# Bias rows written to HBM in 32 shifted copies instead of 128, and read back in parts of 32 partitions

## The chip, the core and the metric

The kernel runs on one core of a Trainium2 chip. The metric is the device time of one execution in microseconds (us). TensorE does the matmuls, VectorE and ScalarE the elementwise work, and 16 DMA engines move data between HBM and the on-chip memory SBUF. DMAs are issued by SyncE (most of them) and by ScalarE; in the profile the two issuing queues are called SPq and ACTq.

## The reference

The reference is a transformer block (two attentions, cross attention, a gated feed-forward) followed by a second block with a recurrent mixer and 64 experts. The change concerns the relative bias of the first block's attentions alone. Both attentions, 8 and 4 heads, add to each logit a value that depends on the distance of query and key:

```python
bias_ht = table_a.T.astype(jnp.float32)
logits = logits + bias_ht[h_i[..., None], rel_bucket(dist)]
mask = slot_ok[None, :, :, None] & (dist >= 0)
logits = jnp.where(mask, logits, NEG_INF)
```

So for each head there is one row of 384 numbers by distance (with the mask in it), and query p of a block of 128 needs 256 of them, starting one place further left than query p - 1 does.

## The kernel before

Weights pass through a stream of pages (128 partitions x 2048 floats, 1 MB). SyncE loads a page (line 220); ScalarE copies it rounded (`wh`, line 246) and VectorE takes the difference (`wl`, line 247); TensorE then multiplies in three passes (lines 643 to 645). `ws512` handles a block of 512 output columns with the weights stationary, in two half blocks (chunks) of one page each and 48 matmuls of 256 columns; `ts512` does the same with the activations stationary. The first blocks are `w_in` columns 512, 0, 1024, 2048, 1536 and 2560. The program's order is written out by hand, engine by engine.

The start of the program: `cols`, `xT` and the first `w_in` page are loaded in pieces (lines 474 to 479), then two more pages (482), `x`, `misc`, `diff_lambda`, `bsp` (from `b_spatial`, line 494) and `brow` (from `b_router`, line 496). For the bias, TensorE multiplies the table with a one-hot matrix (line 710), which gives the 12 rows `bv`; VectorE copies them to SBUF (`bvs`, a part of the page `tmp`, line 711). One DMA from ScalarE's queue (line 715) then writes every row 128 times into the HBM scratch `bd`, copy r shifted by r floats. In the loop around it ScalarE and VectorE convert the first activations and the first weight page, slice by slice (`gain`, line 580 and 581, and `split`, line 575 and 576).

After the third block's matmuls in the program, two SyncE DMAs read `bd` back so that partition p holds its row shifted by p: `biasA` for 8 heads, `biasB` for 4 (line 778). Behind them SyncE loads `memT` and `mem` (lines 892, 894) and the further weights. The attention adds `biasA` to the logits (line 809), takes the maxima (811) and exponentials (813), and TensorE transposes the result (832).

A DMA signals its end on one of eight completion semaphores, DMAHW0 to DMAHW7, which the DMAs of both queues take in rotation. A DMA that takes a semaphore waits first until its previous user has landed.

Of the kernel before, what the change touches and what calls it, by code (L numbers as in the profile page):

```python
# [10 lines left out]
F32 = mybir.dt.float32  # L11
# [312 lines left out]
def body(nc, tc, A, OUT, ctx, dbg=None):  # L324
# [8 lines left out]
    dr = ctx.enter_context(tc.tile_pool(name="dr", bufs=1, space=bass.MemoryType.DRAM))  # L333
# [50 lines left out]
    def w3(t, **kw):  # L384
        return t.rearrange("p (a b) -> p a b", **kw)
# [78 lines left out]
    oh, bvs = tmp0[0:33, 0:384], tmp0[0:12, 384:768]  # L464
# [35 lines left out]
    def gcol(key):  # L500
        a, n = COL[key]
        return [cols[:, i:i + 1] for i in range(a, a + n)]
# [71 lines left out]
    def split(hi, lo, src):  # L574
        S.activation(hi, src, AF.Copy)
        V.tensor_sub(lo, src, hi.bitcast(F32))
# [6 lines left out]
    def gain(parts, xT_, g, ks=range(8)):  # L583

        for k in ks:
            sl = slice(k * 256, k * 256 + 256)
            split_scaled(parts[0][:, sl], parts[1][:, sl], xT_[:, sl], g[k])
# [121 lines left out]
    bv = bank("bv")  # L709
    PE.matmul(bv[0:12, 0:384], tab, oh, start=True, stop=True)  # L710
    V.tensor_copy(bvs, bv[0:12, 0:384])
    bd = dr.tile([12, 128, 512], F32, name="bd")
    for i in range(4):
        if i == 2:
            nc.scalar.dma_start(bass.AP(tensor=bd.tensor, offset=bd.offset, ap=[[65536, 12], [513, 128], [1, 384]]),
                                bvs[:, None, :].to_broadcast([12, 128, 384]))
        s = slice(i * 512, i * 512 + 512)
        gain(hT, xT, gcol("mix_norm_g"), (2 * i, 2 * i + 1))
        split(c.hi[:, s], c.lo[:, s], c.raw[:, s])
# [55 lines left out]
    rel(tmp0)  # L775
    run_all(ts512(hT, "w_in", 1024, evac_v(vab[:, 0:1024], fx)))
    for t, h0, n in ((biasT[0], 0, 8), (biasT[1], 8, 4)):
        nc.sync.dma_start(w3(t[:, :n * 256], a=n), bass.AP(tensor=bd.tensor, offset=bd.offset + h0 * 65536 + 127,
                                                           ap=[[512, 128], [65536, n], [1, 256]]))

    def attention(diff, qk_, v, bias, out_cols):
        q, k = w3(qk_[:, 0:1024], a=4), w3(qk_[:, 1024:2048], a=4)
# [351 lines left out]
    def ffn_in():  # L1134
        hv = [w3(h, a=8) for h in nh["h"]]
        for u in range(11):
# [4 lines left out]
            for n in ("w_gate", "w_up"):  # L1141
# [3 lines left out]
                for k in range(8):  # L1145
# [5 lines left out]
                    if k == 3:  # L1151
# [18 lines left out]
                                                ap=[[0, 128], [1, 1024]]))  # L1170
# [6 lines left out]
    for u in range(11):  # L1177
# [3 lines left out]
        for tt, k2 in sorted(parts) if u == 10 else parts:  # L1181
            f = 2 * u + k2
            i, o = divmod(f * 256, 2048)
# [977 lines left out]
    bd = [mset.bank("ed") for n in range(2)]  # L2161
# [88 lines left out]
```

## Time and profile before

| | |
|---|---|
| median of 3 runs | 1227.41 us (1226.05 to 1227.77) |
| the profiled execution's own time | 1227.2 us |
| its span, first to last instruction | 1225.4 us |
| TensorE busy | 1166.3 us |
| VectorE busy | 632.9 us |
| ScalarE busy | 465.9 us |
| moved by DMA | 353.20 MB, mean 288 GB/s |

The span is shorter than the time by what lies around it, 1.8 us. A busy TensorE is not one at its peak: matmuls are pipelined, and the granted clock, 2.4 GHz or 1.2 GHz, stands in the profile as 1.00 or 0.50.

### The profile page before, as it was taken

Reading aid. Unit: us, or ns where it says so; the run is one execution under the profiler, and the core shown is the slowest. Engines: PE = TensorE matmul, PEld = TensorE weight load, DVE = VectorE, ACT = ScalarE, POOL = GpSimd, SP = SyncE. Lnnn points to the kernel's source line nnn. Section 1 sums busy time; section 2 is a strip of 40 time slices with the busy share of each in tenths; the row PEclk is TensorE's granted clock in tenths of the full one; section 3 lists DMA queues with packets and bytes.
Section 4 is the critical chain, followed back from the end, with each engine's and each line's share of the span. In section 5 each row is a group of like instructions: output and inputs, shape, how many; then the busy total and the mean of one; then the engine's idle time right before and its main releaser. Section 6 shows DMA issues by size and latency. Waiting matters only on the chain.

```text
span 1225.4 us, 18528 instructions
## 1 busy us (share of the span) xinstructions
PE 1166.3 (95%) x7391; PEld 837.5 (68%) x7391; DVE 632.9 (52%) x1280; ACT 465.9 (38%) x738; POOL 2.0 (0%) x9
## 2 busy tenths in 40 slices
PE   7989999999999999999999978999999999998986
PEld 6878987689999988998888757444444434442442
DVE  4568856465545446865686656343333323331333
ACT  4446535545534443777445433111111111110121
POOL 0000000000000000000000000000000000000000
PEclk9889999999999999999999988999999999999998
DMA  8853789644554665343355997899999999999994
GB/s 300 252 213 138 264 344 388 241 174 153 190 206 143 228 226 178 118 149 114 139 193 197 361 359 288 336 410 422 422 420 420 421 421 421 420 421 421 421 420 175
DMA packets 55152, 353.20 MB, mean 288 GB/s; under 512 B 6007, under 2 KB 9368, under 8 KB 13848
## 3 DMA queue, kind: packets, MB, share of 16 engines
q1 hardware_dynamic: 51984, 342.90, 70.7%
q10 hardware_dynamic: 3080, 9.10, 2.6%
q8 instruction: 59, 0.97, 0.3%
q14 instruction: 29, 0.24, 0.1%
HBM read 347.51 MB, written 4.46 MB: 287 GB/s over the span
## 4 chain that ended last, share of the span: by engine, by line
PE 70%; DMA 22%; DVE 4%; ACT 2%; issue 1%; SPq 0%; DVEq 0%; ACTq 0%
DMA w<-in_w_expert_gu 11%; PE gu L1940 8%; DMA w<-in_w_expert_down 6%; PE tsb L643 6%; PE tsb L645 6%; PE tsb L644 6%; PE ed L1969 5%; DMA w<-in_w_in 3%; PE ga L1909 3%; PE acc L1979 3%; PE ws L645 2%; PE ws L643 2%; PE ws L644 2%; PE w_up L643 2%; PE w_gate L643 2%; PE w_up L645 2%
## 5 line engine op out<-in xcount | busy, mean ns | idle before, releaser
L247 DVE TENSOR_TENSOR wl<-w,wh 128x1024 fp32r<-128x1024 f32 (+1 forms) x210 | 242.3, 1201 | 95.9 <-ACT wh L246 87.2
L246 ACT ACTIVATE wh<-w 128x1024 fp32r<-128x1024 f32 (+1 forms) x210 | 205.0, 1039 | 66.6 <-DMA w<-in_w_in 31.8
L1940 PE MATMUL gu<-w,xe 128*32 128x512 f32 (+1 forms) x1216 | 201.3, 594 | 11.8 <-DMA w<-in_w_expert_gu 11.8
L1940 PEld LDWEIGHTS gu<-w,xe 128*32 128x32 f32 (+1 forms) x1216 | 61.1, 121 | 147.5 <-issue 115.2
L1969 PE MATMUL ed<-w,hT 128*32 128x512 f32 (+1 forms) x608 | 109.0, 597 | 3.0 <-DMA w<-in_w_expert_down 2.9
L643 PE MATMUL ws<-hi,wh 128*128 128x256 f32 x352 | 104.1, 296 | 3.2 <-ACT wh L246 3.2
L645 PE MATMUL ws<-hi,wl 128*128 128x256 f32 x352 | 102.7, 292 | 1.6 <-DVE wl L247 1.2
L643 PE MATMUL tsb<-wh,hi 128*128 128x512 f32 x256 | 101.5, 397 | 2.1 <-ACT g1r L572 2.1
L644 PE MATMUL ws<-lo,wh 128*128 128x256 f32 x352 | 102.6, 292 | 0.5 <-DVE lo L581 0.5
L645 PE MATMUL tsb<-wh,lo 128*128 128x512 f32 x256 | 99.9, 390 | 0.0
L644 PE MATMUL tsb<-wl,hi 128*128 128x512 f32 x256 | 99.9, 390 | 0.0
L1949 DVE TENSOR_TENSOR hh<-hh,gu 128x256 f32<-128x256 f32 x27 | 11.4, 422 | 148.3 <-ACT hh L1948 148.3
L580 ACT ACTIVATE ey<-ed,ws 128x512 fp32r<-128x512 f32 x54 | 37.1, 687 | 122.4 <-PE ed L1969 122.4
L1948 ACT ACTIVATE hh<-gu 128x256 f32<-128x256 f32 x27 | 10.4, 383 | 188.2 <-PE gu L1940 188.2
L581 DVE SCALAR_TENSOR_TENSOR ey<-ed,ws,ey 128x512 fp32r<-128x512 f32 x54 | 40.5, 751 | 77.7 <-ACT ey L580 77.7
L643 PEld LDWEIGHTS ws<-hi,wh 128*128 128x128 f32 x352 | 70.6, 201 | 6.2 <-ACT wh L246 3.8
L1969 PEld LDWEIGHTS ed<-w,hT 128*32 128x32 f32 (+1 forms) x608 | 29.8, 121 | 64.8 <-issue 50.0
L645 PEld LDWEIGHTS ws<-hi,wl 128*128 128x128 f32 x352 | 70.3, 200 | 2.4 <-DVE wl L247 1.7
L644 PEld LDWEIGHTS ws<-lo,wh 128*128 128x128 f32 x352 | 70.5, 200 | 0.9 <-DVE lo L581 0.8
L1979 PE MATMUL acc<-ey,gt 128*128 128x512 f32 x216 | 60.0, 412 | 0.0
L643 PEld LDWEIGHTS tsb<-wh,hi 128*128 128x128 f32 x256 | 48.2, 188 | 11.8 <-ACT g1r L572 2.5
L1979 PEld LDWEIGHTS acc<-ey,gt 128*128 128x128 f32 x216 | 37.5, 188 | 27.4 <-issue 21.4
(450 smaller groups left out, 2116.5 us busy)
## 6 DMA issues: line engine op xcount, KB each, us to landing
w<-in_w_expert_gu SPq DMA_DIRECT2D x128, 1024.0 KB, 19.8
w<-in_w_expert_down SPq DMA_DIRECT2D x60, 1024.0 KB, 19.7
w<-in_w_in SPq DMA_DIRECT2D x39, 1024.0 KB, 7.0
w<-in_w_ada SPq DMA_DIRECT2D x24, 1024.0 KB, 7.2
w<-in_w_gate SPq DMA_DIRECT2D x11, 1024.0 KB, 4.9
w<-in_w_up SPq DMA_DIRECT2D x11, 1024.0 KB, 6.5
w<-in_w_down SPq DMA_DIRECT2D x11, 1024.0 KB, 5.0
w<-in_w_out SPq DMA_DIRECT2D x8, 1024.0 KB, 6.7
```

The lines of the kernel that those rows point to most:

```text
L246: kb.nc.scalar.activation(c.hi[:, s], c.raw[:, s], AF.Copy)
L247: kb.nc.vector.tensor_sub(c.lo[:, s], c.raw[:, s], c.hi[:, s].bitcast(F32))
L580: S.activation(hi, src, AF.Copy, scale=col)
L581: V.scalar_tensor_tensor(lo, src, col, hi.bitcast(F32), op0=OP.mult, op1=OP.subtract)
L643: PE.matmul(out, l[0], r[0], start=start, stop=False, skip_group_check=free)
L644: PE.matmul(out, l[0], r[1], start=False, stop=False, skip_group_check=free)
L645: PE.matmul(out, l[1], r[0], start=False, stop=stop, skip_group_check=free)
L1909: PE.matmul(b[:, i * w:i * w + w], xs[part][:, tt, dd * 128:dd * 128 + 128], oh_[:, tt, :], start=part + tt == 0, stop=part + tt == 2)
L1940: PE.matmul(b[w * e:w * e + w, :], xe[:, k, w * e:w * e + w], w3(gu[e][k // 4], a=4)[:, k % 4, :], start=k == 0, stop=k == 7, skip_group_c ...
L1949: V.tensor_mul(h, h, b[:, 256:512])
L1969: PE.matmul(b[w * e:w * e + w, :], hT_[:, f * 128 + w * e:f * 128 + w * e + w], w3(dn[e], a=2)[:, f, n * 512:n * 512 + 512], start=f == 0, ...
L1979: PE.matmul(sums[tt, n], gt[:, tt * 128:tt * 128 + 128], y[:, part * 1024 + n * 512:part * 1024 + n * 512 + 512], start=False, stop=stop a ...
```

## The change

`bd` has 32 shifted copies of each row instead of 128. Queries q to q + 31 (q = 0, 32, 64, 96) read the same 32 copies, each time from a start q floats further left, so that each of the two reads becomes four of 32 partitions. The write also stands ahead of the loop now, so it comes before ScalarE's first conversions.

```diff
-    bd = dr.tile([12, 128, 512], F32, name="bd")
+    bd = dr.tile([12, 32, 512], F32, name="bd")
+    nc.scalar.dma_start(bass.AP(tensor=bd.tensor, offset=bd.offset, ap=[[16384, 12], [513, 32], [1, 384]]),
+                        bvs[:, None, :].to_broadcast([12, 32, 384]))
     for i in range(4):
-        if i == 2:
-            nc.scalar.dma_start(bass.AP(tensor=bd.tensor, offset=bd.offset, ap=[[65536, 12], [513, 128], [1, 384]]),
-                                bvs[:, None, :].to_broadcast([12, 128, 384]))
...
     for t, h0, n in ((biasT[0], 0, 8), (biasT[1], 8, 4)):
-        nc.sync.dma_start(w3(t[:, :n * 256], a=n), bass.AP(tensor=bd.tensor, offset=bd.offset + h0 * 65536 + 127,
-                                                           ap=[[512, 128], [65536, n], [1, 256]]))
+        for q in range(0, 128, 32):
+            nc.sync.dma_start(w3(t[q:q + 32, :n * 256], a=n),
+                              bass.AP(tensor=bd.tensor, offset=bd.offset + h0 * 16384 + 127 - q,
+                                      ap=[[512, 32], [16384, n], [1, 256]]))
```

ScalarE's queue at the start, with what each instruction waits for, before:

```order
5 L580 ACTIVATE hi<-xT,cols 128x256 [waits DMAHW2_49,DMAHW0_49]
6 L580 ACTIVATE hi<-xT,cols 128x256
7 L575 ACTIVATE wh<-w 128x512 [waits DMAHW4_49]
8 L580 ACTIVATE hi<-xT,cols 128x256 [waits DMAHW5_49]
9 L580 ACTIVATE hi<-xT,cols 128x256
10 L575 ACTIVATE wh<-w 128x512 [waits DMAHW6_49]
11 L715 DMA bd<-tmp_71 12x128x384 [waits DVE_49]
```

and now:

```order
4 L471 ACTIVATE warm<-warm 128x1 [waits DVE_49]
5 L713 DMA bd<-tmp_71 12x32x384 [waits DMAHW1_49,DVE_49]
6 L580 ACTIVATE hi<-xT,cols 128x256 [waits DMAHW2_49,DMAHW0_49]
7 L580 ACTIVATE hi<-xT,cols 128x256
8 L575 ACTIVATE wh<-w 128x512 [waits DMAHW4_49]
```

The write, with its wait for VectorE's copy (DVE), has moved ahead of the first conversion. It took DMAHW6 before, and takes DMAHW1 now.

SyncE's queue from the small tables to the memory loads, before:

```order
15 L494 DMA bsp<-in_b_spatial 128x4 [waits DMAHW1_49]
16 L496 DMA brow<-in_b_router 128x64 [waits DMAHW2_49]
17 L220 DMA w<-in_w_in 128x2048 [waits DMAHW3_49]
18 L220 DMA w<-in_w_in 128x2048 [waits DMAHW4_49]
19 L220 DMA w<-in_w_in 128x2048 [waits DMAHW5_49]
20 L220 DMA w<-in_w_in 128x2048 [waits DMAHW6_49,DVE_49]
21 L220 DMA w<-in_w_in 128x2048 [waits DMAHW7_49,DVE_49,PE_49]
22 L220 DMA w<-in_w_in 128x2048 [waits DMAHW0_49,DVE_49,PE_49]
23 L778 DMA biasA<-bd 128x8x256 [waits DMAHW1_49,DVE_49,PE_49]
24 L778 DMA biasB<-bd 128x4x256 [waits DMAHW2_49,PE_49]
25 L892 DMA memT<-in_memT 128x2048 [waits DMAHW4_49,DMAHW3_49,DVE_49]
```

and now, the first 22 rows being in the same order:

```order
22 L220 DMA w<-in_w_in 128x2048 [waits DMAHW0_49,DVE_49,PE_49]
23 L778 DMA biasA<-bd 32x8x256 [waits DMAHW1_49,DVE_49,PE_49]
24 L778 DMA biasA<-bd 32x8x256 [waits DMAHW2_49]
25 L778 DMA biasA<-bd 32x8x256 [waits DMAHW3_49]
26 L778 DMA biasA<-bd 32x8x256 [waits DMAHW4_49]
27 L778 DMA biasB<-bd 32x4x256 [waits DMAHW5_49,PE_49]
28 L778 DMA biasB<-bd 32x4x256 [waits DMAHW6_49]
29 L778 DMA biasB<-bd 32x4x256 [waits DMAHW7_49]
30 L778 DMA biasB<-bd 32x4x256 [waits DMAHW0_49]
31 L893 DMA memT<-in_memT 128x2048 [waits DMAHW1_49,DVE_49]
```

Two reads have become eight. With DMAHW6 for `bd`, the load of row 20 was the next to take it, the fourth full `w_in` page after the small tables; with DMAHW1 the next is `bsp` in row 15, and the rows behind it follow in order.

## Rows read from the trace of the kernel before

**Rows 1.** The page, busy time of TensorE, share of the span, instructions
```profile
PE 1166.3 (95%) x7391; PEld 837.5 (68%) x7391; DVE 632.9 (52%) x1280; ACT 465.9 (38%) x738; POOL 2.0 (0%) x9
```
**Rows 2.** Waits of the engines, 0 to 130 us: total us, times, longest us
```profile
ACT wh L246 <- DMA w<-in_w_in: 31.8, 8, 9.6
...
PE ws L643 <- ACT wh L246: 3.2, 1, 3.2
PE pt L832 <- ACT pp L813: 3.2, 1, 3.2
```
**Rows 3.** Waits of SyncE's DMA queue, 0 to 130 us
```profile
SPq L220 <- DMA bd<-tmp: 25.1, 1, 25.1
```
**Rows 4.** Timeline of SyncE: start us, duration us, what, count
```profile
10.71 0.33 SPq L494 DMA_DIRECT2D bsp<-in_b_spatial  x1
...
13.98 0.33 SPq L220 DMA_DIRECT2D w<-in_w_in  x1
...
45.45 1.28 SPq L220 DMA_DIRECT2D w<-in_w_in  x3
46.83 0.71 SPq L778 DMA_DIRECT2D biasA<-bd  x1
...
54.41 1.12 SPq L220 DMA_DIRECT2D w<-in_w_in  x2
```
**Rows 5.** Timeline of ScalarE; in brackets the idle time before and its end
```profile
4.91 0.91 ACT L580 ACTIVATE hi<-xT,cols 128x256 fp32r<-128x256 f32 x2 [1.44 <-DMA xT<-in_xT]
...
7.86 0.33 ACTq L715 DMA_DIRECT2D bd<-tmp  x1
...
30.39 2.00 ACT L246 ACTIVATE wh<-w 128x1024 fp32r<-128x1024 f32 x2 [9.28 <-DMA w<-in_w_in]
...
50.40 2.01 ACT L246 ACTIVATE wh<-w 128x1024 fp32r<-128x1024 f32 x2 [8.05 <-DMA w<-in_w_in]
...
69.23 2.01 ACT L246 ACTIVATE wh<-w 128x1024 fp32r<-128x1024 f32 x2 [9.59 <-DMA w<-in_w_in]
```
**Rows 6.** Timeline of TensorE, from its first matmuls to the attention's transposes
```profile
6.49 0.58 PE L643 MATMUL ws<-hi,wh 128*128 128x256 f32 x1
...
8.59 0.58 PE L645 MATMUL ws<-hi,wl 128*128 128x256 f32 x1 [0.42 <-DVE wl L576]
...
15.09 0.28 PE L644 MATMUL ws<-lo,wh 128*128 128x256 f32 x1
15.21 0.28 PE L645 MATMUL ws<-hi,wl 128*128 128x256 f32 x1
...
31.50 0.58 PE L643 MATMUL ws<-hi,wh 128*128 128x256 f32 x1 [3.20 <-ACT wh L246]
...
40.46 0.40 PE L643 MATMUL tsb<-wh,hi 128*128 128x512 f32 x1
...
52.77 0.39 PE L645 MATMUL ws<-hi,wl 128*128 128x256 f32 x1 [0.76 <-DVE wl L247]
...
75.93 3.17 PE L832 MATMUL pt<-misc,pp 128*128 128x128 f32 x8 [3.17 <-ACT pp L813]
```
**Rows 7.** Timeline of VectorE: the copy of `bv`, and the first bias addition
```profile
6.59 0.55 DVE L711 COPY tmp<-bv 12x384 f32<-12x384 f32 x1 [5.69 <-PE bv L710]
...
72.60 0.69 DVE L809 TENSOR_TENSOR pp<-qk,biasA 128x512 f32<-128x512 f32 x1
```
**Rows 8.** Windows: stretch, length, busy PE PEld DVE ACT POOL, clock, DMA share, GB/s
```profile
34.00:36.00 2.00, 2.00 (x11) 2.00 (x11) 1.50 (x2) 1.68 (x3) 0.00 (x0) 0.50 0.74 214
76.00:82.00 6.00, 6.00 (x23) 4.58 (x24) 3.60 (x6) 6.00 (x24) 0.00 (x0) 0.51 0.16 66
```
**Rows 9.** DMA: ScalarE's queue 11 to 20, 36 to 44 us; `cols` (KB, us to landing)
```profile
q10 hardware_dynamic: 372, 0.57, 17.1%
...
q10 hardware_dynamic: 405, 0.62, 67.2%
...
cols<-in_cols SPq DMA_DIRECT2D x1, 75.0 KB, 2.0
```

## The prediction

> **What bounds the kernel now.** I first read the page: TensorE is busy 95% of the span [rows 1], so time can only come from stretches in which it stands idle or runs slowly. The change touches the first 60 us alone, so I read the waits of the first 130 us next [rows 2]. TensorE waits long there in two places: 3.2 us before a weight-stationary matmul, for a converted weight page, and 3.2 us before the attention's first transposes, for the exponentials. Behind the first stands ScalarE, which waited 31.8 us in eight pieces for `w_in` pages. The third view is what the DMA queue of SyncE itself waited for [rows 3]: one weight load stood 25.1 us for the write of `bd`. The timeline of SyncE [rows 4] shows it: loads leave at 13.98 us and on to about 20 us, then nothing until 45.45 us, when three loads and the bias reads leave at once.
>
> Why a weight load waits for `bd` is seen in the built order (the section on the change): DMAs take eight completion semaphores in rotation, and each waits for the previous user of its own. Before, `bd` had DMAHW6, whose next user is the fourth full `w_in` load after the small tables. The write itself is slow: alone, its queue moves 405 packets in 8 us, 50 a us, at 67.2% of the engines' time [rows 9], about what 12 busy engines of 16 give. Issued at 7.86 us [rows 5], it holds SyncE until 45.45 us.
>
> TensorE's two stalls follow from late pages. The page that landed at 30.39 us [rows 5] lets TensorE go on at 31.50 us, after 3.20 us idle; the next chunk stage starts at 40.46 us [rows 6], and the granted clock falls to 0.50 after the idle time [rows 8]. The page issued at 54.41 us, behind the bias and memory loads [rows 4], lands at 69.23 us [rows 5]; VectorE must split it before it can add the bias at 72.60 us [rows 7], and the transposes wait until 75.93 us, again with a clock of 0.51 behind them [rows 6, 8].
>
> **The change part by part.**
>
> *A shorter write.* 12 x 32 = 384 packets in place of 1536. The best row is the same queue in the same company: from 11 to 20 us it moved 372 packets [rows 9], so 384 would have been through at about 20.3 us. The new one is issued half a us earlier with the same transfers ahead of it. I take its end as 21 us with the signal. Bounds: alone at 50 packets a us from 11 us, 18.7 us; at half the pace of those 9 us, 29.6 us, which I hold for unlikely since the pace is measured beside full traffic.
>
> *The write goes ahead of ScalarE's first conversions.* It needs the copy of `bv`, which ends at 6.59 + 0.55 = 7.14 us [rows 7]; the first conversion, at 4.91 us before [rows 5], now follows at about 7.6 us. The conversions of one slice took from 4.91 to the first matmul at 6.49 us, so TensorE starts at about 9.2 us. But before, its stream ran without gaps only from 8.59 us [rows 6], since VectorE made that same copy first; the splits for the new stream end near 9.8 us, 1.2 us later. The clock may rise later too; I add 0.7 us for that, about the middle of what is left to 2.7 us. Cost 1.9 us, between 1.2 and the full 2.7. TensorE then ends the third chunk at about 30.2 us instead of 28.3 us (31.50 - 3.20).
>
> *The wait moves to another load.* Now `bd` has DMAHW1, and its next user is the tiny `b_spatial` load, issued at 10.71 us before [rows 4]. It will stand until about 21 us, and `b_router` and the first three weight loads, which left from 13.98 us on, stand behind it. In that time the queue still works off what was issued earlier, so little is lost. The first of them leaves at about 22.2 us. With an empty queue such a page took from 45.45 to 50.40 us, 4.95 us [rows 4, 5]; with 0.8 us for the two small tables it lands at 28 us, against 30.39 us. TensorE went on 1.11 us after the landing (31.50 - 30.39), so the page is ready at about 29.1 us, before TensorE asks for it at 30.2 us. The first stall goes. The following pages are issued right behind it, and TensorE takes 5.8 us for each (below).
>
> What that gives: idle 3.20 us, and the slow chunk behind it. 48 matmuls took 40.46 - 31.50 = 8.96 us; at the spacing of 15.21 - 15.09 = 0.12 us [rows 6] they need 5.76 us. Together 6.40 us; less the late start, 4.5 us.
>
> *Loads four to six, the bias and the memory are freed.* The fourth load leaves at about 24 us instead of 45.45 us, so the 0.76 us wait at 52.77 us [rows 6] goes. The first bias read needs the end of the third chunk, so it leaves at about 30 us instead of 46.83 us [rows 4]. From that issue to the landing at 69.23 us took 22.4 us before, with saturated engines; now that ends at about 53 us. TensorE reaches the transposes 5.3 us earlier, at 67.4 us without a stall (72.76 - 5.3, the stall beginning 3.17 us before 75.93); the landing led them by 75.93 - 69.23 = 6.7 us, so it must come by 60.7 us. There are 7 to 8 us to spare: the second stall goes, 3.17 us, and so does the slow clock behind it. From 76 to 82 us it is 0.51 [rows 8]; half of those 6 us is lost, 3.0 us, and at least 1 us, since part of them waits on exponentials.
>
> *Eight bias reads instead of two.* The bytes are the same. SyncE issues six more at 0.3 to 0.7 us, some 3 us, and the eight take all semaphores, so the last waits for the sixth weight load. The cover is the 7 to 8 us above; I cost it at nothing. The Trainium skill ("DMA: Bandwidth & Descriptors", section "Rules for kernel authors") speaks against this part: transfers to disjoint partition parts share the same engines, and one with all 128 partitions is advised. The `bd` write shows the sharing; no run here shows the split yet.
>
> *Sum*, against this execution's 1227.2 us: -6.4 + 1.9 - 0.8 - 3.2 - 3.0 = -11.5, so **1215.7 us**. The median of the runs, 1227.41 us, is 0.2 us higher. What follows the attention waits for TensorE page by page, so I expect the lead to reach the end.
>
> **The rivals.**
>
> *The first stall stays.* If the write ends at 24 us or later instead of 21 us, its page is ready no earlier than TensorE plus 2 us; from 25 us on the stall is the old one and the clock falls as before. Then only the later half counts: 1227.2 + 1.9 - 0.8 - 6.2 = 1222.1 us. For it: the write's pace depends on its neighbours, and from 11 to 20 us these were large packets. Against: the pace was counted over just the packets that remain.
>
> *Eight small reads cost a landing each.* If they ran one after the other, every added one would take a landing of its own. The nearest row is `cols`, 75 KB, which landed 2.0 us after its issue [rows 9]; six more take 12 us, which exceeds the cover by 4 to 5 us and brings the second stall back: 1215.7 + 6.2 = 1221.9 us. Against: the eight have eight semaphores, so their landings overlap. The Trainium skill ("DMA: Bandwidth & Descriptors", section "Anatomy of one DMA") puts a transfer's fixed cost at about 2.0 us, for the GpSimd path; the row of `cols`, on SyncE's queue, agrees.
>
> *Slower: the new wait holds the first three loads.* Its place is the `b_spatial` load. Every us of the write's end beyond 22 us is a us of idle TensorE before the fourth chunk. With the slow clock behind it (3.2 us), the late start (1.9 us) and the gains left (6.4 + 0.8 + 6.2), the change loses more than 0.2% only if that stall passes 10.8 us, a write that ends after 33 us, say 1231 us at 34 us. Before, 1536 packets ended at 45 us; 384 would have to run at 17 a us. The rows give 41 to 50.
>
> *No change: the lead is lost later.* The last third of the run is limited by expert loads. If their stream were not moved forward, the end would stay at 1227 us. Against: those loads stand in SyncE's order behind all others and wait for pages that TensorE frees.
>
> *More than forecast.* VectorE gets its attention work up to 10 us earlier, and further short waits in the attention may go too: 1211 to 1213 us.
>
> **How the numbers follow.** Forecast with its neighbourhood (1211 to 1219 us) 0.70, first stall stays 0.11, eight reads cost 0.07, more than forecast beyond 1211 us 0.04, no change 0.05, slower 0.03. The range of 8 in 10 goes from 1209 to 1222.5 us: it takes in the two rivals at 1222 us and leaves no change and slower out. A measurement of this kernel tells about 0.2% (2.5 us) from no change, so faster has 0.92, the same 0.05, slower 0.03.
>
> **What would show it.** In the changed profile: the `bd` write ends near 21 us; SyncE waits some 10 us at `b_spatial`, no longer 25 us at a weight load; the page that landed at 30.39 us lands at 27 to 29 us although issued 8 us later; the granted clock stays at 1.00 from about 16 us through 100 us; TensorE starts its first stream about 1 us later but has no idle time over 1 us before the transposes. A stall near 30 us with a clock of 0.50 behind it would make the first gain wrong; a landing of the page before the transposes after 61 us, the second; a time above 1223 us with both stalls gone would show that the lead was lost later.

## The result and the profile after

The changed kernel takes **1215.87 us** (median of 4 runs, 1215.79 to 1216.68) against 1226.95 us for the kernel before on the same chip (4 runs, 1226.05 to 1227.77): ratio 0.9905, 95% interval 0.9893 to 0.9917. The prediction was 1215.7 us, faster with a chance of 0.92. The profiled execution took 1215.87 us with a span of 1214.1 us; before these were 1227.2 and 1225.4 us. So the total is met. The way to it is not: TensorE's first stall, which the prediction counted as gone, is still there.

The page after answers to [rows 1]. TensorE is busy 5.3 us less for the same 7391 matmuls, so a part of the gain is faster work and not less idle time:

```profile
PE 1161.0 (96%) x7391; PEld 832.7 (69%) x7391; DVE 632.8 (52%) x1280; ACT 466.0 (38%) x738; POOL 2.0 (0%) x9
```

Waits of the engines after, 0 to 130 us, to be read beside [rows 2] (total us, times, longest us). The first TensorE stall went from 3.2 to 2.1 us. The second, for the exponentials, went; what is left at the transposes is a wait in the second attention, which was 2.09 us long before (its row stands below):

```profile
PE ws L643 <- ACT wh L246: 2.1, 1, 2.1
...
PE pt L833 <- DVE pp L829: 0.8, 1, 0.8
```

Waits of SyncE's queue after, 0 to 130 us, beside [rows 3]. The wait for `bd` moved from a weight load to the small load of `b_spatial` (line 494), and is 11.2 us in place of 25.1 us:

```profile
SPq L494 <- DMA bd<-tmp: 11.2, 1, 11.2
```

Timeline of SyncE after, beside [rows 4] (start us, duration us, what, count). Nothing leaves between 9.63 and 21.20 us. Then the two small tables go, and four weight loads right behind them. The bias reads start at 28.18 us, where the first stood at 46.83 us before, but the load of `memT` behind them leaves only at 44.49 us:

```profile
9.63 0.33 SPq L492 DMA_DIRECT2D tmp<-in_diff_lambda  x1
21.20 0.33 SPq L494 DMA_DIRECT2D bsp<-in_b_spatial  x1
21.57 0.43 SPq L496 DMA_DIRECT2D brow<-in_b_router  x1
22.05 2.21 SPq L220 DMA_DIRECT2D w<-in_w_in  x4
...
28.18 6.60 SPq L778 DMA_DIRECT2D biasA<-bd  x4
...
34.87 8.76 SPq L778 DMA_DIRECT2D biasB<-bd  x4
44.49 0.35 SPq L893 DMA_DIRECT2D memT<-in_memT  x1
```

Timeline of ScalarE after, beside [rows 5]. The write is issued at 7.01 us and the first conversion follows at 7.44 us, 2.53 us later than before. The page of the first stall lands at 29.47 us, only 0.92 us earlier than before; the one that was late for the attention lands at 57.40 us, 11.83 us earlier:

```profile
7.01 0.32 ACTq L713 DMA_DIRECT2D bd<-tmp  x1
7.44 0.91 ACT L580 ACTIVATE hi<-xT,cols 128x256 fp32r<-128x256 f32 x2 [3.97 <-DVE tmp L711]
...
29.47 2.00 ACT L246 ACTIVATE wh<-w 128x1024 fp32r<-128x1024 f32 x2 [8.50 <-DMA w<-in_w_in]
...
57.40 2.00 ACT L246 ACTIVATE wh<-w 128x1024 fp32r<-128x1024 f32 x2 [3.17 <-DMA w<-in_w_in]
```

Timeline of TensorE after, beside [rows 6]. The third chunk ends at 28.10 + 0.38 = 28.48 us, the fourth waits until 30.58 us, and the transposes come at 69.80 us without any idle time in brackets:

```profile
8.91 0.58 PE L643 MATMUL ws<-hi,wh 128*128 128x256 f32 x1 [2.52 <-ACT wh L575]
...
28.10 0.38 PE L555 MATMUL row<-misc,ny 128*128 128x128 f32 x2
30.58 0.38 PE L643 MATMUL ws<-hi,wh 128*128 128x256 f32 x1 [2.10 <-ACT wh L246]
...
38.93 0.40 PE L643 MATMUL tsb<-wh,hi 128*128 128x512 f32 x1
...
50.07 0.28 PE L645 MATMUL ws<-hi,wl 128*128 128x256 f32 x1
...
69.80 1.04 PE L833 MATMUL pt<-misc,pp 128*128 128x128 f32 x8
...
105.75 1.02 PE L833 MATMUL pt<-misc,pp 128*128 128x128 f32 x4 [0.84 <-DVE pp L829]
```

The last row's counterpart before is this one, 11.46 us later; the spans differ by 11.3 us, so in this execution the lead is carried from here to the end almost unchanged:

```profile
117.21 1.02 PE L832 MATMUL pt<-misc,pp 128*128 128x128 f32 x4 [2.09 <-DVE pp L828]
```

Windows after, beside [rows 8]. From 34 to 36 us the granted clock is still 0.50, from 36 to 38 us 0.86; behind the transposes it is 1.00 now, where it was 0.51:

```profile
34.00:36.00 2.00, 2.00 (x11) 2.00 (x11) 2.00 (x4) 1.80 (x3) 0.00 (x0) 0.50 1.00 422
36.00:38.00 2.00, 2.00 (x17) 2.00 (x16) 2.00 (x3) 0.41 (x1) 0.00 (x0) 0.86 1.05 442
...
70.00:80.00 10.00, 10.00 (x86) 9.50 (x85) 9.62 (x21) 4.67 (x9) 0.00 (x0) 1.00 0.58 211
```

### The profile page after: what moved, and what is told of

Its sections match the earlier page's. It is cut to its first block, busy times and chain, and to the rows that moved or that the text cites. A ratio compares the mean times of both kernels' runs of the same rounds, so it can differ in the third digit from the quotient of the medians.

```text
span 1214.1 us, 18537 instructions
## 1 busy us (share of the span) xinstructions
PE 1161.0 (96%) x7391; PEld 832.7 (69%) x7391; DVE 632.8 (52%) x1280; ACT 466.0 (38%) x738; POOL 2.0 (0%) x9
## 4 chain that ended last, share of the span: by engine, by line
PE 79%; DMA 16%; DVE 2%; ACT 1%; issue 0%; SPq 0%; ACTq 0%; DVEq 0%
PE gu L1941 10%; DMA w<-in_w_expert_gu 8%; PE tsb L643 6%; PE tsb L645 6%; PE tsb L644 6%; PE ed L1970 6%; DMA w<-in_w_expert_down 5%; PE ga L1910 3%; PE acc L1980 3%; PE ws L643 3%; PE ws L645 3%; PE ws L644 3%; PE w_up L643 2%; PE w_gate L643 2%; PE w_gate L644 2%; PE w_up L645 2%
## 5 line engine op out<-in xcount | busy, mean ns | idle before, releaser
L1941 PE MATMUL gu<-w,xe 128*32 128x512 f32 (+1 forms) x1216 | 204.9, 602 | 11.4 <-DMA w<-in_w_expert_gu 11.4
L1970 PE MATMUL ed<-w,hT 128*32 128x512 f32 (+1 forms) x608 | 106.4, 597 | 3.0 <-DMA w<-in_w_expert_down 2.9
```

The lines of the kernel that those rows point to most:

```text
L1941: PE.matmul(b[w * e:w * e + w, :], xe[:, k, w * e:w * e + w], w3(gu[e][k // 4], a=4)[:, k % 4, :], start=k == 0, stop=k == 7, skip_group_c ...
L1970: PE.matmul(b[w * e:w * e + w, :], hT_[:, f * 128 + w * e:f * 128 + w * e + w], w3(dn[e], a=2)[:, f, n * 512:n * 512 + 512], start=f == 0, ...
```

## The experiments

The change has three parts: a smaller write, its place ahead of the loop, and eight reads in place of two. The first four runs take them apart. The theory under test: what counts is when the semaphore of `bd` comes free and which load is its next user, and not the bytes of the write as such. The rival: 2.36 MB of scattered writes (0.59 MB after) take engine time from the loads, so that fewer bytes alone bring the gain. The other four runs ask why the first stall stayed. In this batch the kernel before took 1228.66 us (13 runs, 1227.74 to 1230.31).

**move_only: the write ahead of the loop, still with 128 copies and two reads.**

```diff
+    nc.scalar.dma_start(bass.AP(tensor=bd.tensor, offset=bd.offset, ap=[[65536, 12], [513, 128], [1, 384]]),
+                        bvs[:, None, :].to_broadcast([12, 128, 384]))
     for i in range(4):
-        if i == 2:
-            nc.scalar.dma_start(...)
```

> The write keeps its 128 copies and the reads stay two; the write alone moves ahead of ScalarE's first conversions, so that the next user of its semaphore is the b_spatial load. Theory (a DMA holds its semaphore, and the load that takes it next holds everything behind it on SyncE): the write ends near 43 us, b_spatial and the first three weight loads leave only then, the page for the fourth chunk lands near 51 us, TensorE idles about 24 us, and the late second stall goes because the bias loads are early enough by then: about 1241 us (1235 to 1247). Rival (only the bytes on the DMA engines count, the order does not): 1225 to 1229 us.

Measured: 1238.4 us (1236.79 to 1239.18), ratio 1.0079, interval 1.0062 to 1.0096. Slower, by the mechanism of the prediction's slower rival. Waits of SyncE's queue:

```profile
SPq L494 <- DMA bd<-tmp: 32.8, 1, 32.8
```

Timeline, SyncE, ScalarE and TensorE:

```profile
43.02 0.33 SPq L494 DMA_DIRECT2D bsp<-in_b_spatial  x1
...
50.47 2.00 ACT L246 ACTIVATE wh<-w 128x1024 fp32r<-128x1024 f32 x2 [29.25 <-DMA w<-in_w_in]
...
51.58 0.58 PE L643 MATMUL ws<-hi,wh 128*128 128x256 f32 x1 [23.02 <-ACT wh L246]
```

The long write holds the tiny load, all weight loads stand behind it, and TensorE stands for 23.02 us. The loss in the end is about 9.7 us, since the second stall and others go as in the change. The bytes are those of before; the write's place differs, and with it the load that takes its semaphore next.

**size_only: 32 copies and eight reads, the write left in its old place (at i == 2).**

```diff
-    bd = dr.tile([12, 128, 512], F32, name="bd")
+    bd = dr.tile([12, 32, 512], F32, name="bd")
     for i in range(4):
         if i == 2:
-            nc.scalar.dma_start(bass.AP(tensor=bd.tensor, offset=bd.offset, ap=[[65536, 12], [513, 128], [1, 384]]),
-                                bvs[:, None, :].to_broadcast([12, 128, 384]))
+            nc.scalar.dma_start(bass.AP(tensor=bd.tensor, offset=bd.offset, ap=[[16384, 12], [513, 32], [1, 384]]),
+                                bvs[:, None, :].to_broadcast([12, 32, 384]))
...
```

> 32 copies and eight reads as in the change, but the write stays where it was, in the middle of ScalarE's first conversions, so that the next user of its semaphore is again the fourth full weight load. Theory: the write ends near 20.5 us; the first three weight loads leave from 14 us on as in the kernel before, the page for the fourth chunk lands at 25 to 27 us, the first stall goes altogether, and all gains of the change stay: 1211 to 1213 us, 3 to 5 us below the change. Rival (putting the write ahead is a part of the gain, since it ends sooner): 1216 us or more.

Measured: 1214.0 us (1211.38 to 1215.23), ratio 0.9882, interval 0.9865 to 0.9898: the whole gain of the change, and its interval lies beside the change's 0.9893 to 0.9917 with a small overlap. SyncE shows no wait for `bd`. Timelines of SyncE and ScalarE:

```profile
13.92 9.74 SPq L220 DMA_DIRECT2D w<-in_w_in  x6
...
24.17 2.01 ACT L246 ACTIVATE wh<-w 128x1024 fp32r<-128x1024 f32 x2 [3.07 <-DMA w<-in_w_in]
```

The last of the write's packets move between 20 and 21 us, before the fourth weight load needs the semaphore. Six weight loads leave from 13.92 us on, the page lands 5.3 us earlier than in the change, and TensorE has no stall before the second attention. So the place ahead of the loop gives nothing here. But the time forecast, 1211 to 1213 us, was missed by 1 us at the median, and the profiled execution is the fastest of the four (1211.38 us; the others 1213.58 to 1215.23 us), so the trace shows more lead than the median has.

**split_only: each read cut in four, the write as before.**

```diff
     for t, h0, n in ((biasT[0], 0, 8), (biasT[1], 8, 4)):
-        nc.sync.dma_start(w3(t[:, :n * 256], a=n), bass.AP(tensor=bd.tensor, offset=bd.offset + h0 * 65536 + 127,
-                                                           ap=[[512, 128], [65536, n], [1, 256]]))
+        for q in range(0, 128, 32):
+            nc.sync.dma_start(w3(t[q:q + 32, :n * 256], a=n),
+                              bass.AP(tensor=bd.tensor, offset=bd.offset + h0 * 65536 + 127 + 512 * q,
+                                      ap=[[512, 32], [65536, n], [1, 256]]))
```

> The kernel before with its 128 copies and its place of the write; only the two reads are cut into four of 32 partitions each. Theory (the landings of eight reads on eight semaphores overlap, but the last of them waits for the sixth weight page): the second stall grows by what the loads behind lose, 0 to 5 us: 1227 to 1232 us. Rival (each added read costs a landing of 2 us): 12 us more, 1239 us. Second rival (the split costs nothing): 1227 us within 0.2%.

Measured: 1230.75 us (10 runs, 1229.07 to 1232.17), ratio 1.0017, interval 1.0007 to 1.0027: about 2 us slower. Waits of SyncE's queue and of TensorE:

```profile
SPq L220 <- DMA bd<-tmp: 24.3, 1, 24.3
...
PE pt L834 <- ACT pp L815: 5.3, 1, 5.3
```

Timeline of ScalarE:

```profile
70.53 2.01 ACT L246 ACTIVATE wh<-w 128x1024 fp32r<-128x1024 f32 x2 [11.80 <-DMA w<-in_w_in]
```

Without the earlier semaphore the eight reads have no cover: the page that is late for the attention lands 1.3 us later than in [rows 5], and the second stall grows from 3.2 to 5.3 us. The Trainium skill ("DMA: Bandwidth & Descriptors", section "Rules for kernel authors") advises one transfer over all partitions; this run agrees, with a price of 0.07 to 0.27%. The change pays it in SyncE's time and hides it.

**copies_64: the change with 64 copies and parts of 64 partitions**, which doubles the write and halves the number of reads, from eight to four.

```diff
-    bd = dr.tile([12, 32, 512], F32, name="bd")
+    bd = dr.tile([12, 64, 512], F32, name="bd")
...
-        for q in range(0, 128, 32):
+        for q in range(0, 128, 64):
```

> As the change, with 64 copies and two parts of 64 partitions: twice the write. Theory: the write ends near 28.5 us, b_spatial leaves then, the page for the fourth chunk lands near 37 us instead of 29.5 us, TensorE idles 9 to 10 us there instead of 2.1 us with the slow clock behind it, the later gains stay: 1224 us (1221 to 1227), that is about 8 us above the change for 384 more packets. Rival (the time follows the bytes): a third of the way from the change to the kernel before, 1219 to 1220 us.

Measured: 1222.43 us (1220.91 to 1223.68), ratio 0.9951, interval 0.9934 to 0.9967. Waits of SyncE's queue:

```profile
SPq L494 <- DMA bd<-tmp: 17.2, 1, 17.2
```

Timeline, SyncE, ScalarE and TensorE:

```profile
26.96 0.33 SPq L494 DMA_DIRECT2D bsp<-in_b_spatial  x1
...
35.15 2.00 ACT L246 ACTIVATE wh<-w 128x1024 fp32r<-128x1024 f32 x2 [14.33 <-DMA w<-in_w_in]
...
36.25 0.58 PE L643 MATMUL ws<-hi,wh 128*128 128x256 f32 x1 [7.08 <-ACT wh L246]
```

Release, landing and stall move together, as the table below shows. The time alone would not rule out the rival: a third of the way from the change's 0.9905 to 1 is 0.9937, just inside the interval. The page lands 8.19 us after the release here and 8.27 us in the change, where the prediction had 7 us (21 to 28 us) and where a page on an empty queue took 4.95 us before. Part of what keeps the first stall alive thus lies between release and landing, and there stand the two small tables.

The second batch takes these tables out of the way. It ran on another chip than the first, so across the batches ratios are compared and not times. In it the kernel before took 1227.66 us (11 runs, 1226.47 to 1230.42).

**change_again: the change itself, as the base of this batch.**

> The changed kernel as it is, beside the next three on the same chip. Both theories: 0.990 to 0.991 of the kernel before.

Measured: 1215.45 us (1214.32 to 1217.23), ratio 0.9895, interval 0.9881 to 0.991. Timelines of SyncE, ScalarE and TensorE:

```profile
20.87 0.33 SPq L494 DMA_DIRECT2D bsp<-in_b_spatial  x1
...
28.24 2.00 ACT L246 ACTIVATE wh<-w 128x1024 fp32r<-128x1024 f32 x2 [7.08 <-DMA w<-in_w_in]
...
29.35 0.39 PE L643 MATMUL ws<-hi,wh 128*128 128x256 f32 x1 [0.80 <-ACT wh L246]
```

In this second execution of the same kernel the stall is 0.80 us, not 2.10 us, and the granted clock is 1.00 in every window of 2 us from 28 to 40 us. One of these windows:

```profile
34.00:36.00 2.00, 2.00 (x19) 2.00 (x19) 2.00 (x4) 1.15 (x2) 0.00 (x0) 1.00 1.00 422
```

The first stall of the change therefore varies, and a single profile says only that it is there. Nor does the smaller stall make this execution the faster one: it took 1217.23 us, against 1215.87 us for the other, since it lost time later (see the next section).

**tables_late_after: the change, with the two small loads behind the load of `mem`.**

```diff
-    nc.sync.dma_start(bsp, A["b_spatial_2"][0])
...
-    nc.sync.dma_start(brow, ...)
...
+    nc.sync.dma_start(bsp, A["b_spatial_2"][0])
+    nc.sync.dma_start(brow, ...)
```

> The change, with the two small tables (b_spatial, b_router) loaded behind the memory pages instead of ahead of the weight pages, so that the first held load is a weight page itself. Theory (the two tables, not the wait for the write, are what made the held page land 8.3 us after its release instead of 5 us): SyncE is released near 20.5 us as in the change, the page lands near 25.5 us instead of 29.5 us, the first stall (2.1 us and the slow clock behind it) goes: 0.986 to 0.989 of the kernel before, 3 to 4 us below the change. Rival (the wait for the write is the cost, or the late start of ScalarE's conversions): the same time as the change.

Measured: 1212.81 us (1211.66 to 1213.11), ratio 0.9874, interval 0.9859 to 0.9888. Waits of SyncE's queue:

```profile
SPq L220 <- DMA bd<-tmp: 10.4, 1, 10.4
```

Timeline, SyncE and ScalarE:

```profile
20.88 2.97 SPq L220 DMA_DIRECT2D w<-in_w_in  x6
...
25.71 2.01 ACT L246 ACTIVATE wh<-w 128x1024 fp32r<-128x1024 f32 x2 [4.68 <-DMA w<-in_w_in]
```

The release is at the same time as in change_again, but the next user of the semaphore is now the weight load itself. Its page lands 4.83 us after the release, and TensorE's first stall is gone. The runs lie below all of change_again's, by 2.6 us at the median, where 3 to 4 us had been forecast; the two intervals of the ratios still touch (0.9881 to 0.9888). It has the lowest ratio measured, and its interval overlaps that of size_only.

**tables_late_before: the same move of the two tables in the kernel before.**

> The kernel before with its 128 copies and two reads; only the two small tables move behind the memory pages. By the rotation the next user of the write's semaphore is then the sixth weight load instead of the fourth. Theory: SyncE still stands for the write until about 45 us, but with the fourth and fifth load already gone; the page for the fourth chunk lands near 24 to 26 us without the small tables ahead of it, so the first stall goes and the second stays: 0.994 to 0.997 of the kernel before (1220 to 1224 us against 1227). Rival (only the size of the write counts): no change, 0.999 to 1.001.

Measured: 1223.03 us (6 runs, 1222.47 to 1225.26), ratio 0.9963, interval 0.9951 to 0.9974. Waits of SyncE's queue and of TensorE:

```profile
SPq L220 <- DMA bd<-tmp: 25.5, 1, 25.5
...
PE pt L830 <- ACT pp L811: 6.4, 1, 6.4
```

Timeline, SyncE and ScalarE:

```profile
10.98 9.84 SPq L220 DMA_DIRECT2D w<-in_w_in  x5
46.36 0.33 SPq L220 DMA_DIRECT2D w<-in_w_in  x1
...
26.65 2.00 ACT L246 ACTIVATE wh<-w 128x1024 fp32r<-128x1024 f32 x2 [5.06 <-DMA w<-in_w_in]
```

The rotation shifts by two, so the semaphore of `bd` falls to the sixth weight load and no longer to the fourth. The first stall shrinks to 0.17 us with the full 128 copies being written. But the bias reads still leave after 46 us, and the second stall grows to 6.4 us. With the same bytes, move_only loses 9.7 us and this run wins 4.6 us. That rules out the rival that bytes alone set the time. That the bytes cost nothing at all is not shown: every run with fewer of them also frees the semaphore earlier.

**tables_late_size: the same move in size_only**, where nothing waits for `bd` and the tables hold nobody.

> The run size_only (32 copies, the write at its old place) with the two small tables moved behind the memory pages too. Theory: size_only had no idle TensorE left before the attention, so nothing is left to win: within 1 us of size_only, 0.987 to 0.990 of the kernel before. Rival (the tables cost DMA time in any place ahead of the weights): 2 us faster than size_only.

Measured: 1214.26 us (5 runs, 1213.27 to 1217.43), ratio 0.9893, interval 0.9879 to 0.9908, against 0.9865 to 0.9898 for size_only. Its page lands at 24.15 us, there at 24.17 us. Nothing is won, so moving the tables helped only where they stand between a release and a page that is waited for.

The runs in the order of the landing (us); `brow` is the time from the issue of that table to its landing:

| run | release (first load after the wait) | page lands | landing behind release | `brow` | TensorE's first stall |
|---|---|---|---|---|---|
| tables_late_after | 20.88 | 25.71 | 4.83 | not there | none |
| change_again | 20.87 | 28.24 | 7.37 | 4.5 | 0.80 |
| the change | 21.20 | 29.47 | 8.27 | 5.4 | 2.10 |
| copies_64 | 26.96 | 35.15 | 8.19 | 5.2 | 7.08 |
| move_only | 43.02 | 50.47 | 7.45 | 4.4 | 23.02 |

Where `brow` takes longer, the page behind it lands later by the same amount: in all four runs that have it, the landing behind the release is 2.9 to 3.1 us longer than the time of `brow`.

## Why the prediction was right, and where it was not

The total came out 0.2 us from the forecast, and a part of that is luck: two terms at the head of the sum were wrong in opposite directions, later ones made up the rest, and the second execution of the change divides the same total otherwise. Lead of TensorE over the kernel before, from [rows 6] and the same matmuls after, each step the lead's growth. In change_again these matmuls start at 36.23, 47.37, 67.10 and 104.78 us; both columns are taken against the one profiled execution of the kernel before:

| up to | lead | step measured | step in change_again | step predicted |
|---|---|---|---|---|
| start of the next chunk stage, 40.46 to 38.93 | 1.5 | 1.5 | 4.2 | 4.5 (6.4 - 1.9) |
| third matmul of the next block, 52.77 to 50.07 | 2.7 | 1.2 | 1.2 | 0.8 |
| first transposes, 75.93 to 69.80 | 6.1 | 3.4 | 3.4 | 3.2 |
| transposes of the second attention, 117.21 to 105.75 | 11.5 | 5.3 | 3.6 | 3.0 |
| end of the span | 11.3 | -0.2 | -2.5 | 0 |

The two middle steps, the freed loads and the second stall, came as forecast in both.

- **The write's end, 21 us with the signal: right.** SyncE goes on at 21.20 us. The queue's pace beside full traffic, counted over the packets that remain, was the right row to take. move_only and copies_64 give the same picture at 43.02 and 26.96 us.
- **The wait moves to the `b_spatial` load: right**, 11.2 us where "some 10" was written.
- **Late start, +1.9 us: wrong, it cost 0.17 us in this pair of executions.** ScalarE's first conversion is 2.53 us later, but the third chunk ends at 28.48 us where it ended at 28.31 us before. The prediction had the new stream without gaps from 9.8 us on; it is so from 8.91 us, against 8.59 us before. And the full pace came earlier here, not 0.7 us later: matmuls 0.12 us apart run from 12.75 us on, before from 13.66 us on. Until then they stand 0.21 us apart, as they do from 33.3 to 36 us, where the clock is 0.50; yet the clock's column reads 1.00 in these early windows too, so the clock as the cause is argued and not shown. In the ten profiled executions the full pace began between 12.75 and 14.65 us with the write ahead of the loop, and between 11.53 and 14.37 us with it in the old place. So the 0.17 us is chance in part. In the pairs of kernels that differ in the write's place alone, the third chunk ends later with the write ahead, by 0.25 us (move_only against the kernel before), 0.44 us (tables_late_after against tables_late_size) and 0.65 to 0.72 us (both executions of the change against size_only), still well under 1.9 us.

A window of 1 us of the kernel before (the number in the first brackets counts matmuls):

```profile
13.00:14.00 1.00, 1.00 (x8) 1.00 (x7) 0.00 (x0) 0.02 (x1) 0.00 (x0) 1.00 0.95 393
```

The same window after:

```profile
13.00:14.00 1.00, 1.00 (x11) 1.00 (x10) 0.77 (x2) 0.18 (x1) 0.00 (x0) 1.00 1.08 448
```

- **First stall and its slow clock, -6.4 us: wrong, 1.7 us.** The prediction had the page ready at 29.1 us, 1.1 us before TensorE asks for it at 30.2 us. Both sides moved. TensorE asked at 28.48 us, because the late start cost so little, and the page landed at 29.47 us and not at 28 us, so that TensorE went on at 30.58 us. The earlier request makes up 1.7 us of the miss and the later landing 1.5 us. In change_again the page landed at 28.24 us, almost as written, and the stall of 0.80 us comes from the earlier request alone. The idle time and the late start are thus one quantity: TensorE went on 0.9 us earlier than before (2.2 us in change_again), where the two terms together had 1.3 us (3.2 - 1.9). What the sum really lost is the slow clock. The chunk behind the stall took 8.35 us (38.93 - 30.58), with the clock at 0.50 again, where 5.76 us had been written and 8.96 us stood before; in change_again, with the clock at 1.00, it took 6.88 us, 0.76 us of them a wait for VectorE.
- **The two small tables, 0.8 us: too little.** The sum had 7 us from release to landing: 1.2 us until the first weight load leaves, 4.95 us for the page and 0.8 us for the tables. Measured were 7.4 to 8.3 us with the tables in between and 4.83 us without them (table above), so the tables cost 2.5 to 3.4 us. SyncE's issue of them is 0.85 us of that (21.20 to 22.05 us); the rest passes in the engines. The DMA view of the change shows that `brow`, 32 KB, needs 5.4 us with almost nothing else under way, while `cols` with 75 KB takes 1.8 us (4.5 and 2.5 us in change_again); and from 22 to 26 us the engines move little (DMA share 0.25 and 0.53, the second last number of the windows). The DMA issues of the change (KB, us from issue to landing), 0 to 70 us:

```profile
cols<-in_cols SPq DMA_DIRECT2D x1, 75.0 KB, 1.8
...
brow<-in_b_router SPq DMA_DIRECT2D x1, 32.0 KB, 5.4
```

Windows of the change:

```profile
22.00:24.00 2.00, 2.00 (x19) 2.00 (x18) 0.97 (x6) 0.00 (x0) 0.00 (x0) 1.00 0.25 30
24.00:26.00 2.00, 2.00 (x19) 2.00 (x18) 0.00 (x0) 0.00 (x0) 0.00 (x0) 1.00 0.53 196
```

  The Trainium skill ("DMA: Bandwidth & Descriptors", section "Rules for kernel authors") says that a transfer under 64 KB is mostly overhead. The row of `brow` agrees, with 4.4 to 5.4 us for 32 KB in the four executions of the table.
- **Wait of the fourth load, -0.8 us: right in kind.** The 0.76 us in brackets at 52.77 us are gone; the step measured 1.2 us, and the other 0.4 us were not traced. The wait is gone in split_only too, where the loads were released only 0.9 us earlier than before (44.53 us).
- **Second stall, -3.2 us: right.** The page lands at 57.40 us, where 53 us was written and 60.7 us was the limit, and VectorE adds the bias at 60.77 us, 9.0 us ahead of the transposes.
- **Slow clock behind it, -3.0 us: right in kind, too small as a step.** The clock is 1.00 from 70 to 80 us. The stretch to the second attention's transposes gave 5.3 us. Of these 4.1 us were won by the `tsb` matmul at 80.30 us (90.50 us before), against the 3.0 us of the clock, and 1.25 us are the wait in the second attention (2.09 to 0.84 us), which the sum did not have. The 4.1 us are not divided further, and the 1.25 us are no gain of the change: in change_again that wait is 2.04 us, and the stretch gave 3.6 us.
- **Eight reads at nothing: right in the total, because of the cover, but mis-sized.** Six more reads were to cost SyncE some 3 us. `memT` left 16.3 us after the first read (28.18 to 44.49 us), where it had been 3.8 us (46.83 to 50.60 us); 6.1 us of that are waits for weight pages whose semaphores the reads take. Of the cover of 7 to 8 us, 5.7 us were left (69.80 - 57.40 - 6.7). split_only shows the price without the cover, some 2 us.
- **The lead reaches the end: right in this execution,** 11.5 us at 105.75 us and 11.3 us at the end. In change_again 12.4 us became 9.9 us. About 1.3 us went right behind the wait in the second attention, where the clock fell to 0.50; before, it stayed at 1.00 behind a wait of the same length. The other 1.2 us went later and were not traced.

The wait and a window behind it in change_again:

```profile
104.78 1.17 PE L833 MATMUL pt<-misc,pp 128*128 128x128 f32 x4 [2.04 <-DVE pp L829]
...
106.00:108.00 2.00, 2.00 (x9) 1.19 (x9) 0.69 (x2) 0.08 (x1) 0.00 (x0) 0.50 0.00 0
```

A window behind the wait of 2.09 us at 117.21 us in the kernel before:

```profile
118.00:120.00 2.00, 2.00 (x15) 1.52 (x16) 1.37 (x2) 0.50 (x3) 0.00 (x0) 1.00 0.00 0
```

The slower rival described a real mechanism: move_only is that rival, with a release at 43.02 us. There it was the write's length, 32 copies or 128, that decided.

Not settled: why the full pace begins at such different times; why `brow` takes 4.5 us in one execution of the change and 5.4 us in another, which makes up 0.9 us of the 1.3 us between their first stalls (0.3 us more is the release); and what the late start costs in the total (tables_late_after and tables_late_size differ in it, and their intervals overlap).

## What to carry to other kernels

Where DMAs take completion semaphores in rotation, a slow one holds whatever load comes one round later, with the whole queue behind it; look up that next user before moving or shortening a slow transfer. Make the slow transfer shorter before making it earlier: here the shortening alone gave the whole gain, and the move alone cost 0.8%. And when a queue is released, what stands first in it should be the page that is waited for, not small loads of many packets that nobody needs yet.

## What was not expected of the hardware

- A load of 32 KB into 128 partitions (`brow`) took 4.4 to 5.4 us from issue to landing with the engines nearly empty, where a load of 75 KB took 1.8 to 2.5 us, and it and its smaller neighbour hold the 1 MB page behind them for 2.5 to 3.4 us. The issue alone, 0.85 us for both, hides that.
- ScalarE's first conversion 2.53 us later moved the end of TensorE's third chunk by 0.17 us only. The matmuls came to their full pace anywhere from 11.53 to 14.65 us in ten executions, and among those with the write in the same place that end spreads by 0.7 to 0.95 us, more than the place itself moved it (0.25 to 0.72 us).
- A stall of 0.80 us in change_again had a granted clock of 1.00 behind it to 40 us; one of 2.10 us in the change was followed by 0.50 from 34 to 36 us. The length alone does not tell: in the second attention a wait of 2.04 us in change_again was followed by 0.50 from 106 to 108 us, and one of 2.09 us before by 1.00.
